# Another order of the first tasks of a hybrid attention layer, and a shorter lead of the scores where attention begins

## The chip, the cores and the metric

The kernel runs on one core of a Trainium2 chip. The metric is the time of one execution in microseconds on the device; the median of three runs stands for a kernel. A core has a matrix engine (TensorE, called PE in the profile, its weight loads PEld), a vector engine (VectorE, DVE), an engine for functions and copies (ScalarE, ACT), a slower general one (GpSimd, POOL), and a queue that issues the transfers (SyncE, SP). Each of them runs its own list of instructions in order, and waits where an instruction needs what another engine or a transfer has not finished. Matmuls write to PSUM, a small memory of a few banks; a bank is free again when another engine has copied its contents away.

## What is computed

One layer of a generator over 1024 latent tokens and 256 context tokens, of width 1024. Cut to what matters:

```
mod = silu(c) @ w_ada + b_ada                      # shift, scale, gate
h   = rms_norm(x) * (1 + scale) + shift            # latents and context
p   = h @ w_in                                     # eleven parts
# branch A: gated linear attention, 4 heads, two directions
la_f = log_sigmoid(lr_f @ w_dec[0] + b_dec[0]) / 16   # decay, forward
la_b = log_sigmoid(lr_b @ w_dec[1] + b_dec[1]) / 16   # decay, backward
o_gla = bidir_gla(q, k, v, la_f, la_b, states of the context)
# branch B: differential attention, 8 heads
a = softmax(q1 k1^T) - lam * softmax(q2 k2^T);  o_diff = a @ v
# merge
y = sig(m_gla) * (A @ w_br_gla) + sig(m_diff) * (B @ w_br_diff)
x = x + gate * (y @ w_out)
```

`A` and `B` are the two branches' outputs, normalised and multiplied with their own gates. `lr` is a part of `p` of rank 16 for each direction; the decay is computed from it by one small matmul for each head and direction, and by `log_sigmoid(z) = min(z, 0) - ln(1 + exp(-|z|))`.

## The kernel before, in words

Precision is kept by splitting each float operand into a high part, which the matrix engine takes at its fast float32 rate, and a rest; a product is three matmuls (high by high, high by rest, rest by high). So each operand costs a copy on ACT (the high part) and a subtraction on DVE (the rest), called a split.

The work stands in generators (tasks), one for each strand of the computation. A small planner, the class `Driver`, runs them while the program is written: each operation that a task issues is given a cost, from which the planner keeps a clock for PE (`now`) and for each other engine, and a time at which each tile is ready. A task yields the time or event it waits for, and is due about one microsecond ahead of that. Among the tasks that are due at the same moment the one with the lowest number `prio` goes first. So the order in which the tasks run is the order of the instructions in each engine's list. The clock moves only when PE is given work. `yield d.on("ACT", x)` gives the turn away until `x` is ready and ACT's list has less than about a microsecond left. A tag such as `mm` (three PSUM tiles), `g5` (six tiles of SBUF) or `x4` (one tile) has a fixed number of buffers; `acq` waits for one, `rel` gives it back, and if several tasks wait, the lowest `prio` gets it.

Stages, in order of time:

- The prologue (`prologue`, prio -1): modulation vectors, normalised input, its transposes and its split `h`.
- The first projections (`stream`, prio 9): two column blocks of `w_in`, `gk` and `gq`, in tiles of 128x512. Each tile takes 24 matmuls, into one of the three tiles `mm`, and ends with a copy `p<-mm` on ACT (`post_gk`, `post_gq`, started with prio -1). The weights come through the tile `raw` and are split to `w<-raw` (`wstream`, prio 3).
- Beside them: `job_lr` projects the low-rank part (48 matmuls, three tiles of PSUM, prio 8); `job_la` computes the decay from it (prio 3); `job_gate` computes the gate vector from eight loads of `w_ada` through the one buffer `x4`, with passes on DVE and one small matmul for each of two halves (prio 2); `sums` adds pairs of blocks of `h` for the pair products and stores them (`d_s`, prio 3).
- `job_la` works in four batches (two directions, two pairs of heads). A batch has six small matmuls `l,l` into the PSUM tiles `gs`, `go` and `gt`; for each, ACT writes the absolute value and DVE the minimum with zero (`g<-gs,col` and so on); then ACT makes two exponentials of 128x1280, then two logarithms (`g<-g` on ACT); then DVE subtracts, and the result is stored to `d_la`. A batch takes four of the six tiles `g5`; `sums` takes two.
- The pair products (`pairs`): four more column pairs, by a scheme with seven block products in place of eight. Their weights come through `raw`, `x2`, `l5` and `x4` (`pair_weights`, prio 3). Beside them `presums` prepares sums of `w_out` in four blocks, through `l5` and `x4`; they are scaled with the gate vector, and so wait for `job_gate`.
- Gated linear attention (GLA, four heads), which starts when pairs, decay and `presums` are done, with more projections as filling.
- Differential attention, 64 tiles of 128 queries, when GLA is done. A tile has scores S (two components, 12 matmuls), maxima on DVE, exponentials on ACT, a mix of both components on DVE, transposes T in three groups, a split of these on ACT and POOL, and for each two tiles a product A with the values. PE does S, T and A strictly in the order that `att_order` writes down; matmuls of other projections (`mb`, one PSUM bank, task `fill`) go in between where nothing else is due.
- The output: the second branch's projection and the last product, again in pairs.

The lines of most operations in the profile are those of helpers: L349 is the matmul helper, L375 the transpose, L201 any operation of ACT, DVE and POOL, L314 a transfer. Tiles are therefore told apart by name; a buffer number and a digit behind the name are left out, so `x4` shows as `x`, `g5` as `g`, `l5` as `l`.

Of the kernel before, what the change touches and what calls it, by code (L numbers as in the profile page):

```python
# [22 lines left out]
S = 1024  # L23
CTX = 256
T = S + CTX
# [207 lines left out]
class Hybrid:  # L233
# [596 lines left out]
    def phase_a(self):  # L830
        d = self.d
        self.win = self.a["w_in"][0]
        self.ev_h = {(k, half): Event() for k in range(NK) for half in range(3)}
        self.hx = [[[None] * 2 for _ in range(NK)] for _ in range(2)]
        self.hc = [[None] * NK for _ in range(2)]
        self.ev_plr, self.ev_lr, self.ev_la, self.ev_gb, self.ev_lg, self.ev_sg = [Event() for _ in range(6)]
        self.ev_rope = [Event(), Event()]
        self.ev_gla, self.ev_stream = Event(), Event()
        self.gla_done, self.gla_free, self.gla_back, self.gla_intra, self.gla_sf = (
            [Event() for _ in range(4)] for _ in range(5))  # L840
        self.gla_k = {(x, e): Event() for x in range(4) for e in range(2)}
        self.ev_st = {(nm, c, i): Event() for nm in ("gg", "dq", "dg", "dk") for c in range(2)
                      for i in range(10 if nm == "dk" else 8)}
        allt = list(range(10))
        ctx1 = [8, 9, 0, 1, 2, 3, 4, 5, 6, 7]
        x8 = list(range(8))

        def nat(c0, tiles, post):
            return [(c0 + c * 512, lambda wd, n, c=c: self.job_nat(wd, n, tiles[c], lambda i, pm: post(c, i, pm)))
                    for c in range(2)]  # L850

        def tra(c0, halves, post, ns=4):
            return c0, lambda wd, n: self.job_tr(wd, n, halves, post, ns)

        dk = nat(C_DK, (allt, ctx1), lambda c, i, pm: self.post_qk(1, c, i, pm))
        gg = nat(C_GG, (x8, x8), lambda c, i, pm: self.post_gate(0, c, i, pm))
        dq = nat(C_DQ, (x8, x8), lambda c, i, pm: self.post_qk(0, c, i, pm))
        jobs = [tra(C_GK, [0, 2, 1], self.post_gk), tra(C_GQ, [0, 1], self.post_gq)]
        late = [dk[0], dk[1], dq[0], dq[1]]
        NM = 2  # L860
        for m in range(NM):
            late.insert(2 + 3 * m, tra(C_MG + m * 512, [0, 1], lambda s, half, pm, m=m: self.post_m(4 * m + s, half, pm),
                                            self.NS if m else 4))
        self.fill_from = 4 + self.NS


        self.ev_wl, self.ev_wc = [Event() for _ in range(2)], Event()
        wd = self.wstream([(self.win, j[0]) for j in jobs], "w", (*self.ev_wl, self.ev_wc))
        self.wload = wd.loaded
        self.ev_pl, self.ev_pw, self.ev_zl = Event(), Event(), Event()  # L870
        last = wd[len(jobs) - 1, NK - 1]
        wp = self.pair_weights([c for _, c in self.BY7], wd.loaded[-1], last)
        wd2 = self.wstream([(self.win, j[0]) for j in late], "w", after=(self.ev_zl, self.ev_pw))
        self.wlast = wd2.loaded[-1]

        def stream():
            for n, j in enumerate(jobs):
                yield from j[1](wd, n)
            yield from self.pairs(wp)
            d.spawn(self.to_gla(), prio=-3)  # L880
            for n, j in enumerate(late):
                if n == self.NR:
                    d.spawn(self.rope_tables(0), prio=2)
                yield from j[1](wd2, n)
            d.set(self.ev_stream)

        self.done = {}
        d.spawn(self.prologue(), prio=-1)
        d.spawn(stream(), prio=9)
        d.spawn(self.prep_lr(), At(60.0), prio=2)  # L890
        d.spawn(self.job_lr(), prio=8)
        d.spawn(self.job_la(), prio=3)
        d.spawn(self.consts_late(), At(105.0), prio=2)
        d.spawn(self.job_gate(), At(70.0), prio=2)
        d.spawn(self.sums(), prio=3)

# [459 lines left out]
    def job_la(self):  # L1358

        nc = self.nc  # L1360
        yield self.ev_lr
        _, dws, lrs, _ = self.lr

        def pre(bcol, pm, et, mt):
            yield self.act.activation(et, pm, AF.Abs, bias=bcol)
            return self.dve.tensor_scalar(mt, pm, bcol, 0.0, ALU.add, ALU.min)

        def part(tg, *args):
            e = yield from pre(*args)
            self.rel(tg, e)  # L1370

        for e in range(2):
            for hh in range(2):
                ex, mn = [], []
                yield from self.acq("g5", 4)
                if e and hh:
                    self.d.set(self.ev_lg)
                for h in (2 * hh, 2 * hh + 1):
                    bcol = self.col[:, 16 + e * 4 + h:17 + e * 4 + h]
                    et = self.t("g5", [P, T])  # L1380
                    mt = self.t("g5", [P, T])
                    for half in range(3):
                        o, n = self.hspan(half)
                        tg = ("gs", "go", "gt")[half]
                        yield from self.acq(tg)
                        pm = self.t(tg, [P, 512])
                        en = self.mm(pm[:, :n], dws[:, (e * 4 + h) * P:(e * 4 + h + 1) * P], lrs[:, o:o + n], True, True)
                        self.d.spawn(part(tg, bcol, pm[:, :n], et[:, o:o + n], mt[:, o:o + n]), en)
                        yield AtPE(0)
                    for tg in ("gs", "go", "gt"):  # L1390
                        yield from self.acq(tg)
                        self.free[tg] += 1
                    yield self.d.when(et, mt)
                    ex.append(et)
                    mn.append(mt)
                for j in range(2):
                    self.act.activation(ex[j], ex[j], AF.Exp, scale=-1.0)
                for j in range(2):
                    self.act.activation(ex[j], ex[j], AF.Ln, bias=1.0)
                for j in range(2):  # L1400
                    yield self.d.when(ex[j])
                    self.dve.tensor_tensor(mn[j], mn[j], ex[j], ALU.subtract)
                    self.store([(self.d_la[e][2 * hh + j], mn[j])], ("g5", 2))
        self.rel("l5", self.d.now, 2)
        self.d.set(self.ev_la)
# [502 lines left out]
            self.V[hd] = V  # L1908
            self.d.set(self.ev_v[hd], self.d.when(*V))

    LEAD, AHEAD0 = 4, 3

    def att_order(self):

        S = lambda u: [("S", u, 0), ("S", u, 1)]
        T = lambda u: [("T", u, g) for g in range(3)]
        A = lambda p: [("A", p, 0), ("A", p, 1)]
        order = sum((S(u) for u in range(self.AHEAD0)), [])
        for o in range(-1, 65, 2):
            t, a, s = T(o + 1), A((o - 1) // 2), S(o + self.LEAD + 1)  # L1920
            order += T(o) + S(o + self.LEAD) + [t[0], a[0], t[1], a[1], s[0], t[2], s[1]]
        top = dict(S=64, T=64, A=32)
        order = [x for n, x in enumerate(order) if 0 <= x[1] < top[x[0]] and x not in order[:n]]
        self.turns, self.ev_turn = order, {x: Event() for x in order}
        self.d.set(self.ev_turn[order[0]])
# [876 lines left out]
```

## Time and profile before

| | us |
|---|---|
| median of three runs | 1622.63 (1622.59 to 1624.02) |
| the profiled execution | 1627.62 |
| its span, first to last instruction | 1625.9 |
| PE busy in the span | 1597.1 |
| DVE busy | 1226.6 |
| ACT busy | 836.2 |
| POOL busy | 635.6 |

The mean granted clock of PE over the profiled execution is 0.996. The stages in the span of the profile: the prologue reaches to about 80 us, the first projections with the decay to 173, the pair products to 520, GLA to 910, attention from 910 to about 1456, and the rest is the output.

How to read the rows. In a timeline a row is a run of like instructions: start, length, engine, line, operation, output and inputs, shape, and count (x39). In brackets stands how long the engine was idle ahead of it, and what it waited for. In the table of waits a row says who waited for whom: microseconds in total, times, longest. A row of the windows has, for a stretch of time, the busy time and count of PE, PEld, DVE, ACT and POOL, then the granted clock of PE (1.00 is full), the share of the DMA engines, and GB/s. In the list of transfers stand count, size, and the median time from issue to landing.

### The profile page before, as it was taken

The page shows a single profiled execution, that of the slowest core. Times are in us where ns is not written, and L with a number is a line of the kernel's source. Part 1 is how long each engine was busy: PE and PEld are TensorE (multiplying, and loading weights), DVE is VectorE, ACT ScalarE, POOL GpSimd, SP SyncE. Part 2 cuts the span into 40 slices and gives each one's busy share as a digit, 9 for nine tenths or more (in the row PEclk, how much of TensorE's full clock was granted, in tenths as well). Part 3 has the DMA queues.
Part 4 walks back from the last instruction along what each step waited for, and adds up shares of the span by engine and source line. Part 5 has one row for each costly group of instructions (what it writes and reads, how often), then busy time and mean ns, then how long its engine had stood idle before and what let it go on. Part 6 is the DMA issues. An engine that isn't in the chain of part 4 may idle for free.

```text
span 1625.9 us, 24368 instructions
## 1 busy us (share of the span) xinstructions
PE 1597.1 (98%) x8229; PEld 1331.9 (82%) x8229; DVE 1226.6 (75%) x2117; ACT 836.2 (51%) x1719; POOL 635.6 (39%) x663
## 2 busy tenths in 40 slices
PE   7999999999999999999999999999999999999999
PEld 2687888888788888888888878888888888888887
DVE  4776955467677778867677687888887888888994
ACT  4756633435343354546445466665665655656431
POOL 1400000001314657544555066666665666660000
PEclk9999999999999999999999999999999999999999
DMA  8666798887867558574535854545588455348662
GB/s 295 221 237 233 267 345 312 272 311 272 302 200 264 171 163 251 161 227 133 174 116 153 224 155 128 139 119 157 147 261 243 141 140 161 111 144 292 199 205 103
DMA packets 259565, 331.16 MB, mean 204 GB/s; under 512 B 22600, under 2 KB 160752, under 8 KB 259440
## 3 DMA queue, kind: packets, MB, share of 16 engines
q1 hardware_dynamic: 259440, 329.60, 63.6%
q8 instruction: 65, 1.06, 0.3%
q14 instruction: 60, 0.49, 0.1%
HBM read 225.20 MB, written 104.33 MB: 203 GB/s over the span
## 4 chain that ended last, share of the span: by engine, by line
PE 88%; DVE 5%; DMA 2%; ACT 2%; POOL 1%; issue 1%; SPq 0%; ACTq 0%; DVEq 0%; POOLq 0%
PE mm L349 30%; PE mb L349 10%; PE s L349 8%; PE mc L349 7%; PE b L349 6%; PE tp L349 6%; PE gt L349 5%; PE b L375 4%; PE gs L349 4%; PE go L349 4%; PE mz L349 2%; DVE sm L201 2%; PE tp L375 2%; POOL at L201 1%; DMA w<-in_w_ada 1%
## 5 line engine op out<-in xcount | busy, mean ns | idle before, releaser
L349 PE MATMUL mm<-w,h 128*128 128x512 f32 x912 | 231.0, 400 | 0.0
L349 PE MATMUL mb<-h,wt 128*128 128x512 f32 x840 | 223.8, 401 | 0.0
L201 DVE TENSOR_REDUCE sm<-s 128x1 f32<-128x1024 f32 (+1 forms) x192 | 193.1, 1035 | 10.2 <-PE s L349 4.3
L201 ACT ACTIVATE e<-s,sm 128x1280 f32<-128x1280 f32 x128 | 169.4, 1329 | 56.4 <-DVE sm L201 55.6
L349 PEld LDWEIGHTS mm<-w,h 128*128 128x128 f32 x912 | 167.4, 188 | 32.7
L201 POOL TENSOR_TENSOR at<-ac,at 128x512 fp32r<-128x512 f32 x128 | 187.1, 1462 | 10.7
L349 PE MATMUL mm<-h,w 128*128 128x512 f32 x672 | 173.8, 409 | 3.5 <-ACT p L201 3.4
L201 POOL TENSOR_SCALAR at<-ac 128x512 fp32r<-128x512 f32 x128 | 100.4, 784 | 189.1 <-ACT ac L201 188.9
L349 PEld LDWEIGHTS mb<-h,wt 128*128 128x128 f32 x840 | 151.0, 188 | 28.2 <-DVE ft L201 0.3
L349 PE MATMUL s<-hk,aq 128*128 128x512 f32 x744 | 169.4, 364 | 2.1 <-ACT e L201 2.0
L349 PEld LDWEIGHTS mm<-h,w 128*128 128x128 f32 x672 | 127.1, 193 | 31.1 <-ACT p L201 3.8
L201 DVE TENSOR_TENSOR w<-raw,w 128x512 fp32r<-128x512 f32 x128 | 96.3, 770 | 52.6 <-ACT w L201 51.6
L349 PEld LDWEIGHTS s<-hk,aq 128*128 128x128 f32 x744 | 118.0, 189 | 20.6 <-ACT e L201 5.5
L349 PE MATMUL b<-at,vv 128*128 128x256 f32 x960 | 130.1, 287 | 1.1 <-ACT ac L201 0.8
L349 PEld LDWEIGHTS b<-at,vv 128*128 128x128 f32 x960 | 119.6, 191 | 2.7 <-ACT ac L201 1.0
L201 ACT ACTIVATE ac<-b 128x512 f32<-128x512 f32 x122 | 72.4, 597 | 94.3 <-PE b L375 94.1
L201 DVE SCALAR_TENSOR_TENSOR e<-e,sm,e 128x1280 f32<-128x1280 f32 x64 | 120.0, 1876 | 0.9
L201 POOL TENSOR_TENSOR sm<-sm,nhalf 128x2 f32<-128x2 f32 (+2 forms) x94 | 109.2, 1162 | 27.6 <-DVE sm L201 22.3
L201 ACT ACTIVATE w<-raw 128x512 fp32r<-128x512 f32 x128 | 77.8, 625 | 77.7 <-PE tp L349 21.1
L349 PE MATMUL mm<-w,g 128*128 128x512 f32 x432 | 105.7, 389 | 0.0
L201 POOL TENSOR_TENSOR p<-p,gdif 128x512 f32<-128x512 f32 x12 | 17.4, 1458 | 198.9 <-DVE p L201 174.2
L349 PEld LDWEIGHTS mm<-w,g 128*128 128x128 f32 x432 | 81.1, 188 | 16.8
(353 smaller groups left out, 3125.2 us busy)
## 6 DMA issues: line engine op xcount, KB each, us to landing
raw<-in_w_in SPq DMA_DIRECT2D x62, 512.0 KB, 4.4
g<-d_s SPq DMA_DIRECT2D x32, 640.0 KB, 6.5
g<-d_s SPq DMA_DIRECT2D x32, 512.0 KB, 6.0
aq<-d_qT SPq DMA_DIRECT2D x124, 128.0 KB, 3.6
d_dv<-pl SPq DMA_DIRECT2D x40, 256.0 KB, 3.5
gv<-d_v SPq DMA_DIRECT2D x40, 256.0 KB, 3.3
d_kT<-pl SPq DMA_DIRECT2D x40, 256.0 KB, 2.9
hk<-d_kT SPq DMA_DIRECT2D x32, 320.0 KB, 6.1
```

The lines of the kernel that those rows point to most:

```text
L201: self.ins = f(out, *args, **kw).ins
L349: self.ins = self.nc.tensor.matmul(out, lhsT, rhs, start=start, stop=stop, skip_group_check=more).ins
L375: self.nc.tensor.transpose(out, src, self.ident[:n, :n])
```

## The change

It has three parts. The tasks of the first stage get other priorities: `job_lr` 1 in place of 8, `job_la` 2 in place of 3, `job_gate` 4 in place of 2, `sums` 2 in place of 3. In `job_la`, a `yield` stands between the exponentials and the logarithms of a batch, so that other tasks may put work on ACT's list between them. In `att_order`, two score tiles stand at the very front in place of three; the first two rounds keep the scores three tiles ahead in place of four, and one more score tile is put in at the end of the second round, from where the order is the old one. No arithmetic changes.

Written out, the order of attention was S0 S1 S2 S3, T0 with S4 in between, T1 S5, T2 with A0 and S6 in between, T3 S7, and so on. Now it is S0 S1 S2, T0 with S3 in between, T1 S4, T2 with A0 and S5 in between, S6, T3 S7, and so on.

```
         d.spawn(self.prep_lr(), At(60.0), prio=2)
-        d.spawn(self.job_lr(), prio=8)
-        d.spawn(self.job_la(), prio=3)
+        d.spawn(self.job_lr(), prio=1)
+        d.spawn(self.job_la(), prio=2)
         d.spawn(self.consts_late(), At(105.0), prio=2)
-        d.spawn(self.job_gate(), At(70.0), prio=2)
-        d.spawn(self.sums(), prio=3)
+        d.spawn(self.job_gate(), At(70.0), prio=4)
+        d.spawn(self.sums(), prio=2)
...
                 for j in range(2):
                     self.act.activation(ex[j], ex[j], AF.Exp, scale=-1.0)
+                yield self.d.on("ACT", *ex)
                 for j in range(2):
                     self.act.activation(ex[j], ex[j], AF.Ln, bias=1.0)
...
-    LEAD, AHEAD0 = 4, 3
+    LEAD, AHEAD0 = 4, 2
...
         for o in range(-1, 65, 2):
-            t, a, s = T(o + 1), A((o - 1) // 2), S(o + self.LEAD + 1)
-            order += T(o) + S(o + self.LEAD) + [t[0], a[0], t[1], a[1], s[0], t[2], s[1]]
+            lead = self.LEAD if o >= 3 else self.LEAD - 1
+            t, a, s = T(o + 1), A((o - 1) // 2), S(o + lead + 1)
+            order += T(o) + S(o + lead) + [t[0], a[0], t[1], a[1], s[0], t[2], s[1]]
+            if o + 2 == 3:
+                order += S(o + lead + 2)
```

## The prediction

> **What bounds the kernel now.** I read the page first (busy shares, then the chain that ended last), then the waits of the matrix engine, the windows in which it idled, and the timeline of every engine at those places. The page:
>
> ```profile
> span 1625.9 us, 24368 instructions
> PE 1597.1 (98%) x8229; PEld 1331.9 (82%) x8229; DVE 1226.6 (75%) x2117; ACT 836.2 (51%) x1719; POOL 635.6 (39%) x663
> PE 88%; DVE 5%; DMA 2%; ACT 2%; POOL 1%; issue 1%; SPq 0%; ACTq 0%; DVEq 0%; POOLq 0%
> ```
>
> PE (TensorE) is busy 98% of the span and is 88% of the last chain. The change takes no matmul away. So it can win only two things: idle time of PE, 1625.9 - 1597.1 = 28.8 us in all, and time in which PE works at a lower clock. The waits of PE name its idle time; the first two rows are from 0 to 330 us, the third from after that.
>
> ```profile
> PE tp L375 <- DVE p L201: 4.9, 1, 4.9
> PE mm L349 <- ACT p L201: 3.4, 1, 3.4
> ...
> PE s L349 <- ACT e L201: 2.0, 2, 1.8
> ```
>
> The 4.9 us are transposes of the normalised input in the prologue, whose tasks no edit touches. The 3.4 us lie in the stage with the decay task, the 1.8 us where attention begins: the two places of this change. The windows show what the first costs (columns: window, its length, busy time of PE, PEld, DVE, ACT, POOL with counts, granted clock, DMA share, GB/s):
>
> ```profile
> 126.00:128.00 2.00, 0.00 (x0) 0.00 (x0) 0.33 (x1) 1.99 (x3) 0.00 (x0) 1.00 0.67 216
> 130.00:132.00 2.00, 2.00 (x6) 1.58 (x5) 2.00 (x4) 0.78 (x2) 0.00 (x0) 0.50 1.00 398
> 135.00:136.00 1.00, 1.00 (x6) 0.77 (x5) 0.96 (x2) 0.00 (x0) 0.00 (x0) 0.98 0.79 176
> ```
>
> PE does nothing from 126 to 128 while ACT (ScalarE) is full; afterwards PE counts as busy, but at half the granted clock until 135. The timeline tells who holds whom; PE first, then ACT:
>
> ```profile
> 116.92 9.03 PE L349 MATMUL mm<-h,w 128*128 128x512 f32 x39
> 129.34 11.80 PE L349 MATMUL mm<-h,w 128*128 128x512 f32 x39 [3.38 <-ACT p L201]
> ```
>
> ```profile
> 117.94 0.48 ACT L201 ACTIVATE g<-gt,col 128x256 f32<-128x256 f32 x1
> 121.57 1.15 ACT L201 ACTIVATE w<-raw 128x512 fp32r<-128x512 f32 x2 [3.16 <-DMA raw<-in_w_in]
> 122.63 2.42 ACT L201 ACTIVATE g<-g 128x1280 f32<-128x1280 f32 x2
> 125.08 1.28 ACT L201 ACT_TABLE_LOAD   x1
> 126.37 2.43 ACT L201 ACTIVATE g<-g 128x1280 f32<-128x1280 f32 x2
> 128.71 1.55 ACT L201 ACTIVATE p<-mm 128x512 f32<-128x512 f32 x3
> ```
>
> The projection stream has three PSUM tiles `mm`. Its matmuls end at 125.95; the next needs a tile emptied by a copy `p<-mm`. The copies of the first two tiles, which ended about 24 matmuls earlier (near 120.4), stand on ACT behind the second decay batch: two exponentials, a table load, two logarithms. They run at 128.71, and PE starts 0.63 us later.
>
> **The change, part by part.**
>
> *The yield between Exp and Ln.* It adds no instruction; it adds four points at which the decay task waits, until ACT is within 1 us of the exponentials' end. What is due then goes ahead of the logarithms. In the second batch these are the two finished `p<-mm` copies (task priority -1, the decay's is 3 or 2): two times 1.55/3 = 0.52 us. ACT would run the exponentials to 125.05, the copies to 126.1, then load and logarithms. The first tile is free at about 125.6, before PE asks at 125.95. So the wait of 3.38 us goes. With it goes the half clock behind it: 39 matmuls took 11.80 us after the gap, 39 of the same took 9.03 us before it, a loss of 2.77 us. Behind the yield the logarithms of this batch, their two subtractions and stores come 1.04 us later; they are wanted by the third batch, whose matmuls stand 39 matmuls on. The other three batches hold no PE wait in the rows above, so nothing is won there; there the delay is what counts (the third rival).
>
> Would PE meet the next wait at once? The second column block runs on weights that are all split by 123.7 (the copies at 121.57 are the last), so the 39 matmuls have all they need. The next work that could be late is the gate task's product, and then the pair sums:
>
> ```profile
> 132.61 0.58 SPq L314 DMA_DIRECT2D x<-in_w_ada  x1
> 144.85 0.39 SPq L314 DMA_DIRECT2D x<-in_w_in  x1
> 202.49 0.55 SPq L314 DMA_DIRECT2D g<-d_s  x1
> 225.94 0.81 SPq L314 DMA_DIRECT2D x<-in_w_out  x2
> ```
>
> ```profile
> g<-d_s SPq DMA_DIRECT2D x32, 640.0 KB, 6.5
> ```
>
> ```profile
> 139.78 0.74 DVE L201 SCALAR_TENSOR_TENSOR gb<-x,col,gb 128x512 f32<-128x512 f32 x1
> ...
> 142.85 0.74 DVE L201 SCALAR_TENSOR_TENSOR gb<-x,col,gb 128x512 f32<-128x512 f32 x1
> ...
> 150.77 0.69 DVE L201 TENSOR_TENSOR p<-tp,p 128x512 f32<-128x512 f32 x1 [0.81 <-issue]
> ...
> 266.63 0.68 DVE L201 TENSOR_TENSOR l<-l,l 128x512 f32<-128x512 f32 x1
> ```
>
> ```profile
> 149.65 1.02 PE L349 MATMUL tp<-gb,ones 128*128 128x512 f32 x2
> 210.99 2.20 PE L349 MATMUL mm<-w,g 128*128 128x512 f32 x9
> ```
>
> The last sum of the first pair product lands near 202.49 + 6.5 = 209.0 and is used at 210.99: 2.0 us of slack. What feeds it starts with decay matmuls in PE's order, so it moves forward with PE, and I charge nothing.
>
> *The priorities.* They decide only among tasks due at the same moment. `job_lr` (8 to 1) issues 48 matmuls; on PE only the stream (9) ranks behind it before and after, so PE's order stays: 0, hidden in the same order. `job_la` (24 matmuls, their 48 ACT and DVE passes, 8 Exp, 8 Ln, 8 subtractions, 8 stores) passes the weight stream (3), and so does `sums` (3 to 2). In the second batch that puts the exponentials ahead of the two weight copies at 121.57; these wait for their DMA, and the exponentials' inputs are there from 118.42, so they fill idle ACT time: 0, cover 3.16 us of ACT. If they cover less, it costs nothing as long as the copies are done before PE needs the last two blocks, after 18 of the tile's 24 matmuls (three for each of eight blocks).
>
> `job_gate` (2 to 4) falls behind the weight loads (3). Its eight loads of `w_ada` share one buffer `x4` with a pair weight; the last two DMA rows of that buffer are 132.61 (gate) and 144.85 (pair weight). At rank 4 the pair weight takes the buffer first, and it holds it until the row at 225.94. The gate's eighth load, two DVE passes of 0.74 us, one add and one small matmul then fall behind that: gate done near 226 + 7.2 + 3.8 + 8 + 1 = 246 (its own steps before: load at 132.61, first pass at 139.78, second to 143.6, the add to 151.5, and a last pass of about 1), less the 6 us by which all is earlier, 240. The output-weight sums, which wait for it and took from 225.94 to about 243, end near 257, and give their buffers to weights that DVE first combines at 266.63. Cost 0, covered by about 4 us at first use; if that goes, DVE waits first, not PE.
>
> *Attention.* S is a score tile, T its transposes, A the value product of two tiles. Before: S0 to S3, then T0 with S4, T1, S5, T2 with A0. After: S0 to S2, T0 with S3, T1, S4, T2 with A0 and S5, then S6 at once, T3, S7 as before. The same instructions, moved. At the place:
>
> ```profile
> 910.77 2.58 PE L349 MATMUL s<-hk,raw 128*128 128x512 f32 x12 [0.25 <-ACT p L201]
> ...
> 927.42 0.21 DVE L201 TENSOR_SCALAR sm<-sm,sm 128x1 f32<-128x1 f32 x1
> ...
> 932.76 0.21 DVE L201 TENSOR_SCALAR sm<-sm,sm 128x1 f32<-128x1 f32 x1
> ...
> 938.34 2.40 DVE L201 SCALAR_TENSOR_TENSOR e<-e,sm,e 128x1280 f32<-128x1280 f32 x1
> ...
> 938.94 1.03 PE L375 MATMUL b<-ident,e 128*128 128x128 f32 x8
> ...
> 940.65 1.64 PE L349 MATMUL mb<-h,wt 128*128 128x512 f32 x6
> ...
> 944.11 2.97 PE L349 MATMUL s<-hk,aq 128*128 128x512 f32 x12 [1.82 <-ACT e L201]
> ...
> 945.26 0.59 ACT L201 ACTIVATE ft<-mb 128x512 f32<-128x512 f32 x1
> ```
>
> S5 waits 1.82 us for the softmax of S4, and T2, whose tile is ready, may not pass it; the filler (`mb`) has one bank, full since 942.29. In the new order T2 and A0 stand before S5, so the gap closes: best case -1.82 us. Against it: S5, S6, S7 follow closely. DVE needs 932.76 - 927.42 = 5.3 us per tile here, two tiles 10.7 us; PE has S5, the rest of T2, S6 and T3, 2.6 + 0.3 + 2.6 + 1.3 = 6.8 us (12 matmuls 2.58 us, 8 transposes 1.03). A hole of 3.9 us is left for the filler, which can fill 24 matmuls of 0.228 us, 5.4 us, unless its bank is being emptied. Worst case: -1.82 + 3.9 = +2.1 us. I take -1.0: nearer to the gain, since the filler has half a tile of slack.
>
> **Sum**, against the profiled execution, which took 1627.62 us: -3.38 - 2.77 - 1.0 = -7.15, so 1620.5, 0.44% less. The median of the timed runs is 1622.63, 0.3% below the profiled one; the same share gives 1615.5.
>
> **A rule weighed.** In the rows, 3.38 us of idling was followed by half clock for about 5.7 us, while the 1.82 us at 944 left the clock whole:
>
> ```profile
> 940.00:950.00 10.00, 8.06 (x48) 6.46 (x48) 7.54 (x14) 7.33 (x13) 4.06 (x5) 1.00 0.45 134
> ```
>
> The Trainium skill, "TensorE: Matmul & The Clock Gate", Part 1, says that the clock halves after an idle window of about 3.4 us, and that the windows run free of the kernel. By that, 3.38 us is at the edge: in another execution the same gap may leave the clock alone. The trace agrees that a long gap halves it and a short one does not.
>
> **The rivals.**
> 1. The timed runs never lost the clock, or had a shorter gap: they are 5 us faster than the profiled one, and the gap depends on when a weight landed (121.5 us). A gap short of the bound, as at 944, costs itself alone. Then the gain is between 1.8 and 3.4, plus 1.0: 1618.2 to 1619.8, say 1619. For it: the 5 us. Against: nothing says that they lie here.
> 2. The wait moves to the weights. If the logarithms too go ahead of the last weight copies, these run after load and logarithms: 118.42 + 2.42 + 1.28 + 2.43 = 124.55, then copies and DVE passes to about 127, where PE wants them near 120.4 + 18 x 0.23 = 124.6: a wait of 2.4 us, and with the clock loss again 5.2 us of the 7.15 are eaten: 1617.9 to 1620.6, say 1620.6. Against: the copies `p<-mm` and the weight copies are due while the exponentials run. This is also the case in which the change does not do what it says.
> 3. Slower: the gate's delay reaches the attention of the first branch (GLA). The output-weight sums come in four blocks, one per pair group; if block 0 misses its turn at `x4`, each goes one group later, and the last starts where now it ends:
>
> ```profile
> 467.36 0.81 SPq L314 DMA_DIRECT2D l<-in_w_out  x2
> 495.36 0.32 SPq L314 DMA_DIRECT2D d_pre_t<-x  x1
> 522.29 1.37 SPq L314 DMA_DIRECT2D gk<-d_k  x1
> ```
>
> A block takes 495.36 - 467.36 = 28 us, so it would end near 523 less 6, while GLA, which waits for the block, could start at 522.29 less 6. From there each microsecond may count, since the first score (910.77) waits until GLA is done. Price 0 to 20 us; with the sum above 1615 to 1635, say 1628. It decides if the gate ends after about 285, when the next weights are wanted. For it: the rank. Against: 30 us between 257 and there.
>
> **How the numbers follow.** The forecast holds with 0.58, around 1615.5 (its own range 1612 to 1619); rival 1 with 0.17; rival 2, or an attention loss that eats the rest, with 0.13; rival 3, or another wait made by the new order in the four decay batches, with 0.12. A change of under 0.2% (3.2 us) is about what a measurement can't tell from none. Faster by more: the forecast and two thirds of rival 1 = 0.71; slower: rival 3 and a little of 2 = 0.13; between: 0.16. The range leaves out 3's larger prices: 1611 to 1624.
>
> **What would show it.** Right: no PE wait over 1 us on `ACT p` after 100 us; `p<-mm` between two `g<-g` pairs in the second batch; clock 1.00 from 60 to 160; `x<-in_w_ada` once after 200 us; no `s <- ACT e` wait of 1.8 us near 940. Wrong: a PE wait on `w` near 124, a wait on `g<-d_s` near 205, a gap of over 2 us between S5 and S7, or the first `gk` load later than 517.

## The result and the profile after

The changed kernel takes 1617.92 us in the median of eight runs (1616.47 to 1619.84); the kernel before took 1623.33 beside it (1621.27 to 1626.41). The ratio is 0.9965, with a 95% interval of 0.9955 to 0.9975: by the ratio 5.7 us faster (the two medians differ by 5.4). The forecast of 1615.5 us was 2.4 us too low; the range held.

The page of the kernel after (span, PE's row, the shares of the last chain):

```profile
span 1614.9 us, 24351 instructions
PE 1590.6 (98%) x8229; PEld 1328.0 (82%) x8229; DVE 1223.5 (76%) x2117; ACT 836.2 (52%) x1719; POOL 634.2 (39%) x663
...
PE 91%; DVE 4%; ACT 1%; DMA 1%; POOL 1%; issue 1%; SPq 0%; ACTq 0%; DVEq 0%; POOLq 0%
```

The spans of the two profiled executions differ by 11.0 us, twice what the medians differ by. Part of that isn't the change's. PE comes to the second group of transposes `gt` in the prologue at 25.55 us before and at 24.07 after, and up to there it mostly waits for loads of weights (1.5 us). And some 36 matmuls near 51 us ran partly at half clock before, not after (columns of a timeline: start, length, engine, line, operation, operands, shape, count; first the kernel before, then after):

```profile
51.76 10.92 PE L349 MATMUL mm<-h,w 128*128 128x512 f32 x36
```

```profile
50.53 8.25 PE L349 MATMUL mm<-h,w 128*128 128x512 f32 x35 [1.05 <-DVE h L201]
```

So about 4 us of the 11 are chance of one execution: the run dose_after, below, has the changed kernel's order there, and it too ran at half clock from 50 to 54 us and took 10.05 us for 35 of them. The medians are what counts.

The waits of PE after, first from 0 to 330 us, then from there on:

```profile
PE tp L375 <- ACT p L201: 2.0, 2, 1.0
```

```profile
PE s L349 <- ACT e L201: 1.8, 3, 0.7
PE s L349 <- DVE pl L201: 1.5, 1, 1.5
```

The wait of 3.4 us on `ACT p` is gone (the two of 1.0 left are in the prologue). At attention the two waits on `ACT e`, of 1.8 and 0.2 us, have become three of 1.8 in all, and the first score now waits 1.5 us for the last split of GLA (0.25 us before). The place of the old gap, PE first, then ACT, then a window over it (length, busy time of PE, PEld, DVE, ACT, POOL, granted clock, DMA share, GB/s):

```profile
111.78 21.95 PE L349 MATMUL mm<-h,w 128*128 128x512 f32 x96
```

```profile
113.68 2.44 ACT L201 ACTIVATE g<-g 128x1280 f32<-128x1280 f32 x2
116.00 0.63 ACT L201 ACTIVATE w<-raw 128x512 fp32r<-128x512 f32 x1
116.52 1.09 ACT L201 ACTIVATE p<-mm 128x512 f32<-128x512 f32 x2
117.48 0.65 ACT L201 ACTIVATE w<-raw 128x512 fp32r<-128x512 f32 x1
118.14 1.28 ACT L201 ACT_TABLE_LOAD   x1
119.44 2.44 ACT L201 ACTIVATE g<-g 128x1280 f32<-128x1280 f32 x2
```

```profile
120.00:122.00 2.00, 2.00 (x10) 1.66 (x9) 1.25 (x1) 2.00 (x3) 0.00 (x0) 1.00 0.67 180
```

Two copies `p<-mm` and two weight splits stand between the exponentials and the logarithms. While ACT is full with the logarithms (120 to 122), PE is full too, at full clock: 96 matmuls in one row, where before 39 were followed by a gap and by 39 more that began at half clock.

### The profile page after: what moved, and what is told of

It reads as the page before. It is cut to its first block, busy times and chain, and to the rows that moved or that the text cites. A ratio compares the mean times of both kernels' runs of the same rounds, so it can differ in the third digit from the quotient of the medians.

```text
span 1614.9 us, 24351 instructions
## 1 busy us (share of the span) xinstructions
PE 1590.6 (98%) x8229; PEld 1328.0 (82%) x8229; DVE 1223.5 (76%) x2117; ACT 836.2 (52%) x1719; POOL 634.2 (39%) x663
## 4 chain that ended last, share of the span: by engine, by line
PE 91%; DVE 4%; ACT 1%; DMA 1%; POOL 1%; issue 1%; SPq 0%; ACTq 0%; DVEq 0%; POOLq 0%
PE mm L349 31%; PE mb L349 11%; PE s L349 8%; PE mc L349 7%; PE b L349 6%; PE tp L349 6%; PE gt L349 5%; PE b L375 4%; PE gs L349 4%; PE go L349 4%; PE mz L349 2%; PE tp L375 2%; DVE sm L201 1%; POOL at L201 1%; DMA w<-in_w_ada 1%
## 5 line engine op out<-in xcount | busy, mean ns | idle before, releaser
L349 PE MATMUL mm<-h,w 128*128 128x512 f32 x672 | 168.2, 400 | 1.1 <-DVE h L201 1.1
L349 PEld LDWEIGHTS mm<-h,w 128*128 128x128 f32 x672 | 123.7, 188 | 26.5 <-DVE h L201 1.6
L375 PE MATMUL b<-ident,e 128*128 128x128 f32 x610 | 92.6, 273 | 1.3 <-ACT ac L201 0.8
```

The lines of the kernel that those rows point to most:

```text
L349: self.ins = self.nc.tensor.matmul(out, lhsT, rhs, start=start, stop=stop, skip_group_check=more).ins
L375: self.nc.tensor.transpose(out, src, self.ident[:n, :n])
```

## Experiments

All kernels were timed beside the kernel before; ratios are to that. All but dose_after start from the kernel before. First the parts.

**The yield alone.** The whole of its diff:

```diff
                     self.act.activation(ex[j], ex[j], AF.Exp, scale=-1.0)
+                yield self.d.on("ACT", *ex)
```

> The kernel before with the yield between exponentials and logarithms alone; old priorities, old order of attention. Theory A (the copies behind the second decay batch are the cause): the 3.38 us gap near 126 us and the half clock behind it go, and 3.4 to 6.2 us are won, about 1618. Theory B (the gain comes from the new priorities, since matrix work already stood about 4 to 5 us earlier at 107 us, ahead of that batch): within 1.5 us of the kernel before. Theory C (attention): the same, no change.

Measured: 1631.11 us against 1624.01, ratio 1.0042 (1.0028 to 1.0057). Slower. The wait on `ACT p` is gone as forecast, but PE meets a larger one. Its timeline at the new wait, and the windows around it:

```profile
201.24 0.84 PE L349 MATMUL go<-w,g 128*128 128x512 f32 x3
211.18 3.66 PE L349 MATMUL mm<-w,g 128*128 128x512 f32 x9 [9.10 <-DMA g<-d_s]
```

```profile
205.00:210.00 5.00, 0.00 (x0) 0.00 (x0) 1.12 (x1) 0.00 (x0) 0.44 (x1) 0.72 1.03 357
210.00:215.00 5.00, 3.82 (x11) 3.08 (x12) 0.00 (x0) 1.32 (x3) 0.00 (x0) 0.59 1.00 411
```

PE is ready for the fourth block of pair sums at 202.0, and the first loads of it are issued only at 206.56. This is the place where the prediction counted 2.0 us of slack and charged nothing. The chain behind it: `sums` works block by block on two tiles `g5`. In the third block three of the four splits `x<-g` stand on ACT behind the fourth decay batch (ACT in yield_only):

```profile
162.83 0.75 ACT L201 ACTIVATE x<-g 128x640 fp32r<-128x640 f32 x1
...
165.40 2.44 ACT L201 ACTIVATE g<-g 128x1280 f32<-128x1280 f32 x2
...
172.96 0.72 ACT L201 ACTIVATE x<-g 128x640 fp32r<-128x640 f32 x1
```

The fourth block needs the two tiles back, so its stores start late, at 199.59. In the kernel before all four splits stood ahead of that batch; the last of them, and the batch's exponentials:

```profile
171.35 0.75 ACT L201 ACTIVATE x<-g 128x640 fp32r<-128x640 f32 x1
...
175.95 2.44 ACT L201 ACTIVATE g<-g 128x1280 f32<-128x1280 f32 x2
```

The decay had moved forward with PE; the splits of `sums` had not kept up, and so fell behind it. PE came to the fourth block 9 us earlier than before (202.0 against 210.99; 2.9 us of this lie ahead of 60 us, in the prologue), and the load issued at 202.49 before now comes at 206.56. None of the three theories had this loss.

**The priorities alone:**

```diff
-        d.spawn(self.job_lr(), prio=8)
+        d.spawn(self.job_lr(), prio=1)
-        d.spawn(self.job_la(), prio=3)
+        d.spawn(self.job_la(), prio=2)
-        d.spawn(self.job_gate(), At(70.0), prio=2)
+        d.spawn(self.job_gate(), At(70.0), prio=4)
-        d.spawn(self.sums(), prio=3)
+        d.spawn(self.sums(), prio=2)
```

> The kernel before with the four new priorities alone. Theory A: no change within 1.5 us, and the wait of the matrix engine on the copy p<-mm near 126 us stays. Theory B: 4 to 6 us faster, and the decay's first matmuls stand earlier than 87.4 us. Theory C: no change.

Measured: 1629.51 us, ratio 1.0033 (1.0022 to 1.0044). Slower too, which none of the theories had. It is the mechanism of the second rival, without its half clock, but that rival still left a gain. ACT at the second batch, and PE:

```profile
116.48 2.44 ACT L201 ACTIVATE g<-g 128x1280 f32<-128x1280 f32 x2
...
120.23 2.44 ACT L201 ACTIVATE g<-g 128x1280 f32<-128x1280 f32 x2
122.58 0.61 ACT L201 ACTIVATE w<-raw 128x512 fp32r<-128x512 f32 x1
```

```profile
125.49 0.96 PE L349 MATMUL mm<-h,w 128*128 128x512 f32 x3 [1.52 <-DVE w L201]
```

At rank 2 the whole block goes ahead of the last weight splits, and PE stands in front of the weights. The fourth batch does it again (a wait of 2.54 us on `ACT w` that ends at 172.33), and there the clock was halved behind it (0.50 from 174 to 176).

**The order of attention alone:**

```diff
-    LEAD, AHEAD0 = 4, 3
+    LEAD, AHEAD0 = 4, 2
...
-            t, a, s = T(o + 1), A((o - 1) // 2), S(o + self.LEAD + 1)
-            order += T(o) + S(o + self.LEAD) + [t[0], a[0], t[1], a[1], s[0], t[2], s[1]]
+            lead = self.LEAD if o >= 3 else self.LEAD - 1
+            t, a, s = T(o + 1), A((o - 1) // 2), S(o + lead + 1)
+            order += T(o) + S(o + lead) + [t[0], a[0], t[1], a[1], s[0], t[2], s[1]]
+            if o + 2 == 3:
+                order += S(o + lead + 2)
```

> The kernel before with the new order of the first attention tiles alone. Theory A, with the term of the forecast: 1 us faster. From the profile of the changed kernel (waits of 0.7 and 0.7 us on ACT e, and a gap between 980 and 1000 us): 0.5 to 2 us slower. Theory C: 4 to 6 us faster.

Measured: 1622.54 us, ratio 0.9995 (0.9986 to 1.0004): not to be told from nothing. Windows of 50 us from the first score on, before and then here:

```profile
910.77:960.77 50.00, 47.70 (x250) 38.73 (x251) 41.86 (x66) 29.38 (x49) 17.18 (x15) 1.00 0.70 191
960.77:1010.77 50.00, 49.49 (x306) 42.99 (x305) 41.52 (x76) 31.17 (x65) 34.03 (x29) 1.00 0.52 143
1010.77:1060.77 50.00, 50.00 (x311) 44.01 (x310) 42.67 (x79) 31.94 (x67) 32.50 (x30) 1.00 0.45 122
```

```profile
906.61:956.61 50.00, 48.68 (x260) 40.82 (x261) 41.64 (x67) 28.90 (x50) 16.44 (x15) 1.00 0.74 202
956.61:1006.61 50.00, 48.84 (x300) 42.08 (x298) 41.02 (x74) 30.15 (x62) 33.69 (x29) 1.00 0.49 134
1006.61:1056.61 50.00, 49.47 (x303) 42.74 (x304) 42.71 (x80) 34.22 (x71) 33.70 (x31) 1.00 0.49 138
```

The first 50 us win 0.98 us of PE time, the next two give back 0.65 and 0.53. Idle over 150 us: 2.81 before, 3.01 here. In these two profiles the gain lasts 50 us and is then paid for by later waits. From the first score to the end of the span it is 715.1 us before and 716.0 here; with the early stage changed it is 715.0 with the old order (yield_and_prio) and 715.4 with the new (the changed kernel).

**Yield and priorities together**, with the old order of attention; against the changed kernel the diff is the last one turned round (its first lines):

```diff
-    LEAD, AHEAD0 = 4, 2
+    LEAD, AHEAD0 = 4, 3
...
```

> The changed kernel with the old order of attention put back. Theory A: 4 to 6 us faster than the kernel before, and if the new attention order costs something, 0.5 to 2 us faster than the changed kernel (about 1617). Theory C: like the kernel before.

Measured: 1619.56 us, ratio 0.9974 (0.9963 to 0.9985). Two parts that each lose 5 to 7 us win 4 together. From 60 to 330 us PE has no wait on `w`, on `ACT p` or on `g<-d_s`. All four splits of the third block now stand ahead of the fourth batch's exponentials (ACT):

```profile
156.27 0.74 ACT L201 ACTIVATE x<-g 128x640 fp32r<-128x640 f32 x1 [3.64 <-DVE g L201]
...
162.28 0.73 ACT L201 ACTIVATE x<-g 128x640 fp32r<-128x640 f32 x1
...
167.85 2.44 ACT L201 ACTIVATE g<-g 128x1280 f32<-128x1280 f32 x2
```

Which part of the yield, and which rank, does that? The next three kernels take them one by one.

**The yield in the second batch only**, with the old priorities:

```diff
-                yield self.d.on("ACT", *ex)
+                if (e, hh) == (0, 1):
+                    yield self.d.on("ACT", *ex)
```

> The kernel before with the yield in the second decay batch only (forward direction, second pair of heads); old priorities and attention. Theory D: the yield takes the gap on p<-mm away, and with the old priorities its fourth batch makes the pair sums late (the 9.1 us wait on g<-d_s of the yield alone). Then this kernel has neither wait and is 3 to 6 us faster than the kernel before. Rival E: the yield in the second batch already reorders what follows, and the wait on g<-d_s comes back: 1 to 8 us slower.

Measured: 1633.50 us against 1624.48, ratio 1.0047 (1.0031 to 1.0063). PE:

```profile
174.20 4.47 PE L349 MATMUL mm<-w,h 128*128 128x512 f32 x12 [2.01 <-ACT p L201]
...
216.73 3.75 PE L349 MATMUL mm<-w,g 128*128 128x512 f32 x9 [8.68 <-DMA g<-d_s]
```

The wait for the sums stays, so the yields of the other batches don't make it. The one yield that the forecast credited with the whole gain brings it about by letting PE arrive early; three of the four splits stand behind the fourth batch here too (175.01 to 179.20, its exponentials at 167.48). And the fourth batch without a yield now stops PE itself (2.01 us), a wait that the profile of before did not hold.

**The yield and the rank of `sums`** (3 to 2, the other ranks old):

```diff
-        d.spawn(self.sums(), prio=3)
+        d.spawn(self.sums(), prio=2)
```

> The yield in all batches and sums raised from 3 to 2; the other priorities old. Theory D1 (sums behind the weights makes the pair sums late; its new rank heals that): no wait over 2.5 us on g<-d_s, 3 to 6 us faster than the kernel before. Rival D2 (it is the decay's own rank, or the gate's): the wait of about 9 us stays, about 7 us slower, as with the yield alone.

Measured: 1632.08 us, ratio 1.0049 (1.0031 to 1.0066). PE waits even longer, 11.46 us, and here all four splits of the third block stand behind the exponentials of the fourth batch (168.45 to 175.59, the exponentials at 165.15):

```profile
213.61 4.21 PE L349 MATMUL mm<-w,g 128*128 128x512 f32 x9 [11.46 <-DMA g<-d_s]
```

The rank of the late task alone does not heal it.

**The yield and all new ranks but that of `sums`** (`sums` left at 3). Against yield_and_prio:

```diff
-        d.spawn(self.sums(), prio=2)
+        d.spawn(self.sums(), prio=3)
```

> The counterpart: the yield with the new ranks of job_lr, job_la and job_gate, and sums left at 3. Theory D1: the wait on g<-d_s stays, 3 to 8 us slower than the kernel before. Rival D2: no such wait, 3 to 6 us faster.

Measured: 1625.08 us, ratio 1.0004 (0.9992 to 1.0016). The wait for the sums is down to 1.85 us, and one for weights appears:

```profile
169.32 0.50 PE L349 MATMUL tp<-w,h 128*128 128x512 f32 x1 [2.39 <-ACT w L201]
```

So the other ranks do most of it (1.0042 to 1.0004), and the rank of `sums` the rest (to 0.9974). Neither theory had this middle.

**More of the suspected block, before.** Two further passes of 128x1280 on ACT (each tile copied onto itself) between exponentials and logarithms of the second batch, in the kernel before:

```diff
                     self.act.activation(ex[j], ex[j], AF.Exp, scale=-1.0)
+                if (e, hh) == (0, 1):
+                    for j in range(2):
+                        nc.scalar.activation(ex[j], ex[j], AF.Copy)
```

> The kernel before, in the same order everywhere, with two more passes of 128x1280 on ACT between the exponentials and the logarithms of the second decay batch (copies of a tile onto itself). Theory A (the copies p<-mm wait for this block of ACT work): the wait of PE on ACT p grows by 2.4 us from about 3.4 to about 5.8 us, and the time by about 2.4 us (up to 5 where the half clock lasts longer). Rival: the wait is not bound to the block, and neither changes.

Measured: 1627.07 us against 1624.48, ratio 1.0016 (1.0005 to 1.0028): 2.6 us (0.8 to 4.5) for about 2.4 us of ACT. ACT, then PE:

```profile
119.61 2.43 ACT L201 ACTIVATE g<-g 128x1280 f32<-128x1280 f32 x2
```

```profile
128.63 11.79 PE L349 MATMUL mm<-h,w 128*128 128x512 f32 x39 [4.88 <-ACT p L201]
```

The wait was forecast at 5.8 us and is 4.88, 1.5 more than the 3.38 of before. Counted from the start of the exponentials it fits: from there to PE's restart it is 6.7 us in the kernel before (122.63 to 129.34), 6.7 in attention_only (120.81 to 127.52) and 9.0 here (119.61 to 128.63), 2.3 more for 2.4 us of passes. So the block of the decay task causes the gap. How long the gap is depends also on how far ahead of PE's stop the exponentials start: 3.3, 3.9 and 4.1 us.

**The same passes after**, behind the new yield, in the changed kernel:

```diff
                 yield self.d.on("ACT", *ex)
+                if (e, hh) == (0, 1):
+                    for j in range(2):
+                        nc.scalar.activation(ex[j], ex[j], AF.Copy)
```

> The changed kernel with two further passes of 128x1280 on ACT (each tile copied onto itself, so the values are the same) behind the yield of the second batch, ahead of its logarithms: about 2.4 us more on ACT at the place where dose_before got it. There it made the wait on ACT p longer (4.9 us in its profile against 3.4 and 2.8) and the time 2.6 us longer. If the yield has taken the decay's block off the path of PE: no PE wait over 1 us on ACT p near 120 us, and the time within 1 us of the changed kernel, ratio to before 0.996 to 0.9975. If the copies or weight splits behind the logarithms are just in time: a wait of up to 2.4 us on ACT p or on w near 120 to 127 us, ratio 0.998 to 0.999.

Measured: 1618.20 us against 1624.11, ratio 0.9972 (0.9961 to 0.9982); the changed kernel had 0.9965 (0.9955 to 0.9975). PE's row and the passes (L1401):

```profile
114.12 21.95 PE L349 MATMUL mm<-h,w 128*128 128x512 f32 x96
```

```profile
120.33 2.45 ACT L1401 ACTIVATE g<-g 128x1280 f32<-128x1280 f32 x2
```

The 96 matmuls take 21.95 us as without them. Behind the yield ACT has more than 2.4 us to spare here.

**The splits held ahead of the fourth batch.** If the sums are late because their splits stand behind the fourth batch, then putting them ahead, with nothing else changed, must take the wait away. The yield in all batches, old priorities, and:

```diff
+                if e and hh:
+                    yield self.ev_x2s
                 for j in range(2):
                     self.act.activation(ex[j], ex[j], AF.Exp, scale=-1.0)
...
                 self.store([(self.d_s[n, k][:, 0], hi), (self.d_s[n, k][:, 1], o)], ("x2", 1), ev=self.ev_s[n, k])
+            if k == 2:
+                d.set(self.ev_x2s)
```

> The kernel before with the yield in all four batches and the old priorities, and one more thing: the fourth decay batch issues its exponentials only after the third block of pair sums has issued its four splits, so that on ACT these splits stand ahead of Exp, table load and Ln instead of three of them behind. This is an order of issue; no instruction is added, and the arithmetic is the same. In yield_only those three splits ran at 172.96, 174.10 and 175.21, the fourth block's stores began at 199.59, and PE waited 9.1 us for its loads from 202.0 on. Theory F (the wait on g<-d_s comes from the third block's splits standing behind the fourth decay batch on ACT; the fourth block inherits the delay through the two g5 tiles): the splits run by about 167, the fourth block's stores start near 185 to 190, the wait on g<-d_s is under 2 us, and the time falls by 8 to 10 us against yield_only, to about 1621 with the before at 1624, ratio 0.997 to 0.999. Theory G (the chain of the sums is too long for the earlier PE whatever stands on ACT, or the new ranks act in another way): the wait stays at 6 us or more, ratio 1.002 or higher. Theory H (the delay only changes its victim: the fourth batch's logarithms or the copies behind them now hold PE): wait on g<-d_s gone, but a new PE wait of over 2 us on ACT before 200 us, ratio near 1.000.

Measured: 1623.13 us against 1624.11, ratio 0.9992 (0.9983 to 1.0001). Against yield_only (1.0042) that is 0.5% or 8 us back, the lower end of what theory F gave (its ratio, 0.997 to 0.999, is just missed). ACT, then PE:

```profile
171.76 0.73 ACT L201 ACTIVATE x<-g 128x640 fp32r<-128x640 f32 x1
...
174.74 2.44 ACT L201 ACTIVATE g<-g 128x1280 f32<-128x1280 f32 x2
```

```profile
207.76 3.28 PE L349 MATMUL mm<-w,g 128*128 128x512 f32 x9 [1.86 <-DMA g<-d_s]
```

The wait falls from 9.10 to 1.86 us. Theory F holds for most of the wait: these splits' place in ACT's list is its cause. No new wait of over 2 us before 200 us took its place, so H falls. It isn't as good as the new ranks: the first split comes no earlier than in yield_only (166.65 against 162.83, with the first pair product 3.8 us later too), only the batch gives way.

**The rank of the gate left old.** Against yield_and_prio:

```diff
-        d.spawn(self.job_gate(), At(70.0), prio=4)
+        d.spawn(self.job_gate(), At(70.0), prio=2)
```

> The yield and the new ranks of job_lr (1), job_la (2) and sums (2), with the old rank 2 of job_gate and the old order of attention; against yield_and_prio (ratio 0.9974) it tells what the gate's rank is for. If the gate's fall behind the weight loads is only a delay without cost or use, as the prediction had it (cost 0): the same as yield_and_prio, ratio 0.996 to 0.9985, no PE wait on g<-d_s over 1 us. If the gate's DVE passes and its hold on the buffer of a pair weight are part of what makes sums or weights late: a wait on g<-d_s or on w of 2 us or more after 160 us, ratio 0.999 to 1.003. A gate product back near 145 to 150 us in PE's order is expected in both cases.

Measured: 1626.66 us, ratio 1.0018 (1.0009 to 1.0027), against 0.9974 with the gate at 4: the gate's rank is worth about 7 us in this company. The forecast had put it at 0. ACT and PE:

```profile
163.16 2.44 ACT L201 ACTIVATE g<-g 128x1280 f32<-128x1280 f32 x2
...
171.32 0.62 ACT L201 ACTIVATE w<-x 128x512 fp32r<-128x512 f32 x1
```

```profile
171.99 0.50 PE L349 MATMUL tp<-w,h 128*128 128x512 f32 x1 [3.89 <-ACT w L201]
```

A weight split and three splits of the third block fall behind the fourth batch again, and PE waits for the weights. For the sums it waits only 0.70 us here, though these splits stand at 170.69 to 172.99, much as in yield_only: PE has already lost 4.9 us to the weights, and the fourth block's stores begin at 193.11. So the place behind the batch does not fix the wait alone; what else made the fourth block earlier here is not shown.

**The rank of `job_lr` left old.** Against yield_and_prio:

```diff
-        d.spawn(self.job_lr(), prio=1)
+        d.spawn(self.job_lr(), prio=8)
```

> The yield and the new ranks of job_la (2), job_gate (4) and sums (2), with the old rank 8 of job_lr and the old order of attention; against yield_and_prio (ratio 0.9974). In the traces with job_lr at 1 the decay's first matmuls start 82 to 85 us into the span, with job_lr at 8 at 87 to 89 us, so its 48 matmuls stand about 5 us further ahead in PE's order, against what the prediction said (PE's order stays, cost 0). In this kernel the four splits of the third summed block still stand ahead of the fourth batch's exponentials, but the whole decay is some 5 us later against the pair products. If the rank of job_lr is without effect on the end: the same as yield_and_prio, ratio 0.9965 to 0.998, no PE wait over 1 us on g<-d_s. If the earlier decay is part of what makes the sums early enough: a wait on g<-d_s of 1 to 4 us near 205, as in yield_hold (1.9 us), ratio 0.9985 to 1.0005.

Measured: 1621.70 us against 1622.12, ratio 0.9990 (0.9980 to 0.9999). Some of the gain is missing, though the intervals of the two (0.9963 to 0.9985 with the new rank) touch. It isn't where I expected it: no wait on `g<-d_s` near 205. The waits of PE from 0 to 330, and PE in the second pair product:

```profile
PE mm L349 <- DVE hk L201: 0.7, 1, 0.7
```

```profile
403.95 3.70 PE L349 MATMUL tp<-w,g 128*128 128x512 f32 x15 [1.38 <-DMA g<-d_s]
```

Both waits stand in the profile of before too (0.7 and 1.7 us) and in neither yield_and_prio nor the changed kernel. Together they are 2.1 us; against that, yield_and_prio has a wait of 0.7 us on `ACT p` at 380 that is missing here. From the transposes `tp<-ident,g` near 60 us to the first score this kernel takes 843.4 us and yield_and_prio 840.9, about the 2.6 us by which the two ratios differ. My expectation also took the starts of the decay as they stand in the spans, and that misled it: they hold the chance of the prologue, and over all profiles they overlap (82.3 to 85.8 us with `job_lr` at 1, 84.8 to 88.7 with it at 8). Counted from those transposes, the first decay matmul comes 23.7 to 24.0 us later in the six profiles with `job_lr` at 1, and 24.9 to 25.3 in the eight with it at 8. So the rank moves the decay by 1.2 us, not 5.

## Why the prediction was right, and where it was not

- **The gap and its cause: right.** The yield lets the copies past the logarithms, the gap closes; the doses show that the block was the cause before and is off the path after.
- **"So it moves forward with PE, and I charge nothing": wrong.** This step failed. The sums are sums of blocks of `h`: no decay matmul stands in their chain. They have their own list of waits (two `g5` tiles, DVE, ACT), and their loads came 4 us later, not earlier (206.56 against 202.49). With 2.0 us of slack and a PE that was to come over 6 us earlier, a wait was due: 9.10 us in yield_only, 8.68 in yield_batch2, more than the gap had cost. The yield by itself is a loss of 7 us.
- **"The priorities: 0": wrong, twice.** Alone they cost 5 us, by the mechanism of the second rival and a second time at the fourth batch. With the yield they are worth 11 us (1.0042 to 0.9974): they keep splits of sums and weights ahead of the fourth batch, and yield_hold, which puts only the splits of the sums there, brings back 8 of the 11. The terms on the way were wrong as well: "PE's order stays" fails for `job_lr` (the decay comes 1.2 us earlier, and a wait of 0.7 us on `hk` goes), and the gate's rank is not neutral.
- **"The other three batches hold no PE wait": true of that profile only.** Once PE came earlier, the fourth batch stopped it in yield_batch2 and prio_only.
- **The gate's delay: half right.** Its second product came at 241.62, forecast 240, without harm, but the agreement is partly luck: three loads of `w_ada`, not one, fell behind 200 us (213.73, 222.54, 229.11), and the first block of the output-weight sums started at 284.85 instead of ending near 257: it did miss its turn, as the third rival had it. Yet the second block followed at 305.61, and the third and fourth kept their turns, so GLA got its first load at 509.82, early. The price of rival 3 was never paid.
- **Attention -1.0: not confirmed.** Timed alone it is -0.8 us (-2.3 to +0.6), which tells neither -1.0 nor nothing. In the profiles it is a loss of 0.2 us of idle time over 150 us, and of 0.9 and 0.4 us from the first score to the end. The mechanism was another than the prediction's: no hole of 2 us at S5 to S7, but two waits of 0.7 us ahead of them and two of 0.8 and 0.4 us near 1006.
- **The size of the sum.** Forecast -7.15 us; measured -5.7 (interval -7.3 to -4.1). The first rival has its share in this: attention_only, with the early stage unchanged, shows the gap at 2.79 us and no clock loss (39 matmuls in 9.14 us):

```profile
127.52 9.14 PE L349 MATMUL mm<-h,w 128*128 128x512 f32 x39 [2.79 <-ACT p L201]
```

So the old gap cost 2.8 us in one profiled execution and 6.15 in another. Besides, the changed kernel wins 0.7 us on `hk` and 1.0 net on the sums of the second pair product (1.7 less, but 0.7 on `ACT p` at 377 new), and loses 1.2 at the first score. From the rows that makes 3.3 to 6.6 us without a term for attention. Counted directly, from the transposes near 60 us to the first score, it is 848.3 us before, 845.3 in attention_only and 840.9 in the changed kernel: 4.5 to 7.4 us. The measured 4.2 (yield_and_prio, 2.4 to 6.0) and 5.7 agree with that within their intervals.

Two slips, on which nothing rests: the wait of 4.9 us in the prologue is that of PE's very first transpose (40x40, at 4.88 us), not of the normalised input; and the chance of "faster by more" comes to 0.69 by its own terms, not 0.71.

So the total came out right with a chain that was wrong in the middle: two errors, a wait not charged and a cure not credited, cancelled. To that extent it was luck. What stays open: by which of its effects each rank works (a place in ACT's list, the buffer `x2`, or a turn at `g5`), and whether the rank of `job_la` alone matters, which was not tried.

## What to carry to other kernels

A gap closed early in a kernel makes the busiest engine arrive early at every later meeting; a wait of the profile before tells nothing of those that it hid, so for each later transfer ask which engine's list makes it, and whether that list moves forward too. Parts of a change that only reorder are not additive: each alone lost 5 to 7 us here, both together won 4, so time them together and apart before one of them is called neutral. A block of long passes on one engine was cheap here where the passes that feed the critical engine stood ahead of it (2.4 us more of it cost nothing to be seen), and where they stood behind it, each microsecond added to it held them back by about as much (2.3 us for 2.4).

## What was not expected of the hardware

The clock does not follow the length of the gap alone. A gap of 2.79 us (attention_only, above) left it whole, and so did 1.82 us in the kernel before. But 1.85 us (yield_rest, ending at 208.50), 1.86 us (yield_hold) and 2.01 us (yield_batch2) were followed by half clock. Windows behind the gaps of attention_only, of yield_batch2 (at 172) and of yield_hold (at 206):

```profile
128.00:130.00 2.00, 2.00 (x11) 1.62 (x10) 2.00 (x4) 0.96 (x2) 0.00 (x0) 1.00 0.91 364
```

```profile
176.00:178.00 2.00, 2.00 (x6) 1.56 (x5) 2.00 (x4) 0.90 (x2) 0.00 (x0) 0.50 1.01 388
```

```profile
210.00:212.00 2.00, 2.00 (x6) 1.61 (x5) 0.00 (x0) 1.05 (x2) 0.00 (x0) 0.50 1.06 428
```

Twelve matmuls took 4.47 us behind the gap of yield_batch2 and 2.88 elsewhere, so a gap of 2 us cost 3.6. The Trainium skill, "TensorE: Matmul & The Clock Gate", Part 1, has the clock halve after an idle window of about 3.4 us, with windows that run free of the kernel. That the same place in the prologue, near 50 us, is hit in one execution (dose_after, behind a gap of 1.01 us) and spared in another (the changed kernel, behind 0.95 us) agrees with free windows; that gaps of 1.9 us were enough does not, since they are too short to hold an idle window of 3.4. What decides is not shown. The prediction's sentence that a gap short of the bound "costs itself alone" is therefore not safe: here a PE gap of 1.85 to 4.9 us costs itself and sometimes up to 2.8 us more.
